# One-hot operands that interleave two tokens instead of four

## The chip, the cores and the metric

The kernel runs on one core of one Trainium2 chip. The metric is the device time of the program in microseconds (us). The kernel before took 1945.64 us, the median of three runs (1944.63 to 1948.22).

The engines are TensorE (PE in the profile, its weight loads PEld), VectorE (DVE), ScalarE (ACT), GpSimd (POOL) and the DMA queue of SyncE (SP).

## The reference

A decoder trunk of two layers on 256 tokens of 1024 columns, float32. Each layer has an attention mixer and then a PEER mixer, which takes most of the time. PEER works on product keys: 8 heads, for each two halves of 128 sub-keys, and 128 x 128 = 16384 experts of one neuron each.

```python
q = (xc @ w_q).reshape(t, PEER_HEADS, 2, PEER_QDIM // 2)
sc = jnp.einsum('thpc,hpnc->thpn', q, sub_keys).astype(jnp.float32)
v_half, i_half = lax.top_k(sc, PEER_TOPK_HALF)
...
top_s, pos = lax.top_k(cand, PEER_TOPK)
expert = jnp.take_along_axis(cand_idx, pos, axis=-1)
g = jax.nn.softmax(top_s, axis=-1)
u = u_tab[expert]
act = jax.nn.gelu(jnp.einsum('thkd,td->thk', u, xc).astype(jnp.float32), approximate=False)
w = (g * act).astype(xc.dtype)
return jnp.einsum('thk,thkd->td', w, v_tab[expert])
```

## The kernel before

The kernel does not gather experts. It multiplies the tokens with all 16384 rows of `u_tab`, applies gelu, multiplies by a dense matrix of gates that is zero where an expert was not chosen, and multiplies that with all of `v_tab`. An expert's number is (row, column) of a 128 x 128 table; the first half of the keys gives the row, the second the column.

`peer(layer, ...)` runs once per layer, in these stages:
- the queries: 16 tiles of `w_q`, each two halves of 12 matmuls in `split_prod` (L804 to L806), and the top-16 searches and the routing on VectorE (`stage1`, `stage2`);
- the u stage: 128 blocks `b` of 128 experts, each two halves of 12 matmuls of 256 columns (L804 to L806), into a PSUM tile `S`. `put_act` (L1010, L1011, L1013) takes a block from PSUM through gelu into the array `A`;
- the v stage: 128 blocks, 24 matmuls of 512 columns each (`mm`, L1072 to L1074).

All these products are in float32r, with every operand split in hi + lo: hi hi, lo hi and hi lo. The halves of the weights come through `Weights.split`: one DMA of 512 KB for two halves, then per half ScalarE rounds hi (L69) and VectorE subtracts for lo (L70), five buffers each.

The gate matrix is made in the generator `gates()`, whose steps `Background.pump` issues between the matmuls of the u stage. Each step handles four tokens, `t0` to `t0 + 3`, and its tiles come from the pool `ohp` with two buffers:
- `hot` builds four one-hot operands. `E` (bfloat16, tile `ohB`) is [128 slots, 2, 128 indices, 4 tokens]: the partition is one of the 128 (head, rank) slots of a token, the two planes are the one-hot of the row and of the column index. `G` (float16, tile `ohA`) has the row's one-hot times the two parts of the gate's mantissa, `RM`.
- VectorE compares `iotaX` with the indices in `R1` (L959 for both planes, L957 for the first alone) and multiplies (L963, L966; L970 for the gate's exponent). In every other step (`GA`) ScalarE makes the second plane, token by token: a square (L953) and a relu (L951).
- Then the gate products: for each of the four tokens and each of the two planes of `G` one matmul (L984), 128 columns of `G` against 128 columns of `E`, into a PSUM tile `scp`. This is a group of eight.
- ScalarE copies the result to `A` (L992), or VectorE multiplies it into blocks that `put_act` has already been to (L996).

The tokens are the innermost dimension of `E` and `G`, so that VectorE handles four neighbours with four different factors, and the columns of one token's operand lie four 2-byte elements, 8 bytes, apart. The gate groups lie in the u stage: 64 in each layer, 128 in all.

The program is recorded by a framework whose scheduler sets each engine's order when the kernel is built; the work is then in that order on each engine.

Of the kernel before, what the change touches and what calls it, by code (L numbers as in the profile page):

```python
# [38 lines left out]
class Weights:  # L39
    """The weights in the order of use: units of up to 1024 columns are loaded ahead of  # L40
    the products, and split in halves into float32r parts hi + lo = w."""
# [33 lines left out]
    def next(self, look=None):  # L75
        """the next half: (hi, lo)"""
        j = self.pos
        self.pos += 1
        self.split(j + (self.look if look is None else look))
        return self.parts.pop(j)  # L80

    def last4(self, products):
        """products(half, tb) of the next 4 halves (hi, lo): all for tb 0, then all for tb 1"""
# [10 lines left out]
class Background:  # L94
    """Streams of work (generators that yield the cost of each step) that is issued
    between the matrix products of the main stream."""
# [20 lines left out]
    def need(self, *names):  # L117
        """issue the streams of these names to their ends"""
# [25 lines left out]
def body(tc, I, out):  # L144
    nc = tc.nc
    with ExitStack() as ctx:
# [58 lines left out]
        iotaX = cp.tile([128, 128, 4], BF, name="iotaX")  # L205
        nc.vector.tensor_copy(iotaX, iota[:, :, None].to_broadcast([128, 128, 4]))
# [41 lines left out]
        def rsqrt(parts, n, name):  # L248
            """parts: columns [128, k] that add up to the sums of squares over n -> 1 / sqrt(mean + eps)"""
# [9 lines left out]
            # Newton's steps, y times -2, 16 and -8192 after them: y (3 - v y^2) / 2  # L259
# [10 lines left out]
        def x_rstd(scr, tbs=(0, 1)):  # L270
            """1 / rms of the tokens of the blocks tbs -> [128, len(tbs)]"""
# [12 lines left out]
        def to_T(src, c, col, hi, lo, psp, tag):  # L284
            """chunk c, src(tb, c) [128, 128] -> hi[c], lo[c] transposed, times the gain"""
# [7 lines left out]
        def product(hi, lo, cs, n, w, ps, first, last):  # L293
            """ps[tb] [128, n] += (hi+lo)[c][:, tb].T @ the half's chunks, c in cs"""
# [14 lines left out]
        def proj(name, hi, lo, chunks, n, per, psp, consume, pre=None):  # L309
            """one tile of n output columns; `per` chunks in each half"""  # L310
# [11 lines left out]
        def rope(dst, ps, nh, d, C_, S_, tb, tmpp):  # L322
            """dst [128, nh, d] = rope(ps [128, nh*d])"""
# [13 lines left out]
        def scaled(tables, r, ap, name):  # L337
            """rope tables times the tokens' factors r [128, 2]"""
# [8 lines left out]
        def attention(hs, qk, scale, vof, masks, ap, oT, psp, need1, need2):  # L347
            """a group of 4 heads. qk(h, qb, nk) -> (lhsT, rhs); vof(h, kc) -> V [128 keys, 64];
            oT (hi, lo): 8 chunks [128, 256]"""
# [78 lines left out]
        class OutProj:  # L428
            """x += (oT hi + lo).T @ w_out, chunk after chunk in the same accumulators"""
# [24 lines left out]
            def finish(self, cs):  # L454
                bg.need(*[f"A{c // 2 * 4}" for c in cs])
                """the last two chunks, and x += the sums"""
# [27 lines left out]
        def heads_T(dsts, tabs, psp, tmpp):  # L484
            """rope over 8 heads of 64 columns, then transposed to dsts = [(dst, scale, chunks)]"""
# [20 lines left out]
        # ---------------------------------------------------------------- layer 0 mixer  # L506
# [120 lines left out]
        # ---------------------------------------------------------------- layer 1 mixer  # L627
        def mla_mixer(gcol):
            with ExitStack() as c1:
# [28 lines left out]
                def put_c(j):  # L658
                    """columns 352j.. of [cq 768 | ckv 256 | kr 32]"""
# [28 lines left out]
                def put_heads(j, dst, tail, rname, out_):  # L688
                    """8 heads [t, 64 + 32] -> out_[j] [96, 8, 256]"""
# [54 lines left out]
        # ---------------------------------------------------------------- PEER  # L744
        def peer(layer, gcol, final=False):
            with ExitStack() as c1:
                pp = c1.enter_context(tc.tile_pool(name="pp", bufs=1))
                # the activations: the blocks from NA on take the place of the raw tokens
# [13 lines left out]
                R1, RM = hp.tile([128, 3, S], BF, name="R1"), hp.tile([128, 2, S], F16, name="RM")  # L762
# [19 lines left out]
                # the queries come from the raw tokens times the gain: 1 / rms goes to their scores  # L782
# [25 lines left out]
                def finish():  # L808
                    """the last norm, in the places of the loaded weights"""
# [15 lines left out]
                def top16(srcs, vals, idxs):  # L825
                    """the 16 largest of each source and their places, the sources in turn"""
# [17 lines left out]
                def stage2():  # L844
# [5 lines left out]
                    for tb in range(2):  # L850
                        v = V[:, tb].rearrange("p (h s) k -> p h s k", s=2)
                        # only pairs (a, b) with (a + 1)(b + 1) <= 16 can be among the 16 largest sums
# [13 lines left out]
                    # softmax over the 16; the first is the largest  # L866
# [3 lines left out]
                    for tb in range(2):  # L870
                        g, tpu = gs[:, tb], tps[:, tb]
                        iv = If[:, tb].rearrange("p (h s) k -> p h s k", s=2)
                        # place -> (a, b): the last row that starts at or before it
# [9 lines left out]
                        # (a + 1)(b + 1) - 1 pairs come before (a, b): the k-th has a and b up to k  # L883
# [31 lines left out]
                        nc.scalar.activation(R1[:, :2, ts], p[:, :2], AF.Copy)  # L915
# [3 lines left out]
                    # g = 2^e (m + r): m has 11 bits, r the rest  # L919
# [6 lines left out]
                    nc.scalar.activation(R1[:, 2], e2, AF.Copy)  # L926
# [10 lines left out]
                def gates():  # L937
                    def hot(t0, E, G):
                        t = slice(t0, t0 + 4)
                        bc = lambda r: r[:, None, t].to_broadcast([128, 128, 4])  # L940
# [5 lines left out]
                        def pair(i, relu):  # L946
                            if act:
                                for j in (i, i + 1):
                                    r = [RA[:, n, k + j:k + j + 1] for n in range(3)]
                                    if relu:  # L950
                                        nc.scalar.activation(e[:, :, j], e[:, :, j], AF.Relu, bias=r[1], scale=r[2])  # L951
                                    else:
                                        nc.scalar.activation(e[:, :, j], iota, AF.Square, bias=r[0], scale=-1.0)  # L953
# [200 lines left out]
```

## Time and profile before

| | us |
|---|---|
| median of three runs | 1945.64 |
| lowest, highest | 1944.63, 1948.22 |
| span of the profiled execution | 1945.3 |

The profiled execution has no time of its own beside the span; its span lies 0.3 us under the median of the runs.

The page's share of busy time is a mean over stages with different limits. The gate products lie between 322 and 628 us (layer 0) and between 1277 and 1582 us (layer 1); these two stretches are called gate stages below. Matmuls are pipelined, so their durations overlap: what a matmul costs in a row of others is read from the chain of waits, where each piece is the time from the end of the one before, and not from its own duration.

### The profile page before, as it was taken

To read this page: it belongs to the slowest core of one execution; us is meant where nothing else is said; L and a number is where in the kernel's file an instruction comes from. 1 tells how busy PE (TensorE), PEld (TensorE's weight loads), DVE (VectorE), ACT (ScalarE), POOL (GpSimd) and SP (SyncE) were. 2 spreads that over 40 slices of the span, in tenths; PEclk is the share of its full clock that TensorE was granted. 3 is DMA by queue.
4 is the path that set the end of the run, shared out by engine and by line. 5 is a ranking of instruction groups with operands and counts; after the bars stand their busy time and mean duration, and the time that the engine had idled before them with its cause. 6 is when DMAs were issued, how large, how long until landed. Compare 5 with 4: busy or idle time off the path is not lost.

```text
span 1945.3 us, 35740 instructions
## 1 busy us (share of the span) xinstructions
PE 1917.9 (99%) x12588; PEld 1727.7 (89%) x12588; DVE 1454.4 (75%) x3710; ACT 1264.2 (65%) x3060; POOL 6.4 (0%) x10
## 2 busy tenths in 40 slices
PE   8999999999999999999999999999999999999997
PEld 7769999999999888888888799999999998888886
DVE  7958998777788666666687699977778876666665
ACT  5556567887777555555576664688877765555554
POOL 0000000000000000000000000000000000000001
PEclk9989999999999999999999999999999999999999
DMA  6425565444444555555554345654444456666664
GB/s 186 128 65 164 172 195 166 154 151 152 152 152 153 194 192 190 192 192 190 189 168 131 120 150 177 195 163 152 144 152 152 154 171 191 190 194 193 188 193 141
DMA packets 90179, 323.33 MB, mean 166 GB/s; under 512 B 10512, under 2 KB 10896, under 8 KB 89744
## 3 DMA queue, kind: packets, MB, share of 16 engines
q1 hardware_dynamic: 88704, 318.71, 51.4%
q8 instruction: 99, 1.62, 0.3%
q0 software_dynamic: 288, 2.10, 0.3%
q14 instruction: 80, 0.66, 0.1%
q10 hardware_dynamic: 1008, 0.25, 0.1%
HBM read 319.97 MB, written 1.05 MB: 165 GB/s over the span
## 4 chain that ended last, share of the span: by engine, by line
PE 94%; DVE 3%; DMA 1%; ACT 1%; issue 1%; ACTq 0%; DVEq 0%
PE S L804 13%; PE S L805 13%; PE S L806 13%; PE acc L1072 12%; PE acc L1073 12%; PE acc L1074 12%; PE scp L984 6%; PE pj L301 2%; PE pj L303 2%; PE pj L302 2%; PE bk L372 1%; DVE lo L70 1%; DMA raw<-in_pu 1%; PE pj L438 1%; PE scp L1021 1%; PE pj L439 1%
## 5 line engine op out<-in xcount | busy, mean ns | idle before, releaser
L69 ACT ACTIVATE hi<-raw 128x512 fp32r<-128x512 f32 (+2 forms) x1214 | 763.2, 634 | 589.8 <-DVE lo L70 196.5
L70 DVE TENSOR_TENSOR lo<-raw,hi 128x512 fp32r<-128x512 f32 (+2 forms) x1214 | 827.1, 686 | 377.4 <-ACT hi L69 368.5
L804 PE MATMUL S<-hi,hi 128*128 128x256 f32 x2048 | 584.2, 285 | 1.9 <-ACT A L1013 1.8
L806 PE MATMUL S<-hi,lo 128*128 128x256 f32 x2048 | 573.4, 280 | 0.5 <-DVE lo L70 0.3
L805 PE MATMUL S<-lo,hi 128*128 128x256 f32 x2048 | 572.9, 280 | 0.0
L804 PEld LDWEIGHTS S<-hi,hi 128*128 128x128 f32 x2048 | 389.4, 190 | 3.1 <-ACT A L1013 2.9
L806 PEld LDWEIGHTS S<-hi,lo 128*128 128x128 f32 x2048 | 386.4, 189 | 1.3 <-DVE lo L70 1.2
L805 PEld LDWEIGHTS S<-lo,hi 128*128 128x128 f32 x2048 | 387.3, 189 | 0.0
L1073 PE MATMUL acc<-lo,ohA 128*128 128x512 f32 x512 | 200.2, 391 | 0.0
L1073 PE MATMUL acc<-lo,ohB 128*128 128x512 f32 x512 | 200.2, 391 | 0.0
L1074 PE MATMUL acc<-hi,ohA 128*128 128x512 f32 x512 | 199.4, 390 | 0.0
L1074 PE MATMUL acc<-hi,ohB 128*128 128x512 f32 x512 | 198.7, 390 | 0.0
L1072 PE MATMUL acc<-hi,ohB 128*128 128x512 f32 x512 | 160.5, 393 | 0.0
L1072 PE MATMUL acc<-hi,ohA 128*128 128x512 f32 x512 | 160.5, 393 | 0.0
L984 PE MATMUL scp<-ohA,ohB 128*128 128x128 f16 x1024 | 143.1, 296 | 0.0
L951 ACT ACTIVATE ohB<-ohB,RA 128x128 bf16<-128x128 bf16 x256 | 134.5, 654 | 0.0
L1074 PEld LDWEIGHTS acc<-hi,ohB 128*128 128x128 f32 x512 | 96.1, 188 | 22.0
L1074 PEld LDWEIGHTS acc<-hi,ohA 128*128 128x128 f32 x512 | 96.1, 188 | 22.0
L1072 PEld LDWEIGHTS acc<-hi,ohA 128*128 128x128 f32 x512 | 96.2, 188 | 20.8
L1072 PEld LDWEIGHTS acc<-hi,ohB 128*128 128x128 f32 x512 | 96.2, 188 | 20.7
L1073 PEld LDWEIGHTS acc<-lo,ohA 128*128 128x128 f32 x512 | 96.2, 188 | 20.3
L1073 PEld LDWEIGHTS acc<-lo,ohB 128*128 128x128 f32 x512 | 96.2, 188 | 20.2
(263 smaller groups left out, 2524.8 us busy)
## 6 DMA issues: line engine op xcount, KB each, us to landing
raw<-in_pu SPq DMA_DIRECT2D x256, 512.0 KB, 3.6
raw<-in_pv SPq DMA_DIRECT2D x256, 512.0 KB, 4.1
raw<-in_pq SPq DMA_DIRECT2D x32, 512.0 KB, 3.5
raw<-in_w SPq DMA_DIRECT2D x20, 512.0 KB, 3.7
raw<-in_uq SPq DMA_DIRECT2D x9, 512.0 KB, 4.3
raw<-in_w SPq DMA_DIRECT2D x12, 352.0 KB, 2.9
raw<-in_w0o SPq DMA_DIRECT2D x8, 512.0 KB, 3.6
raw<-in_w1o SPq DMA_DIRECT2D x8, 512.0 KB, 3.5
```

Of the source, the lines that this page charges most:

```text
L69: self.nc.scalar.activation(hi[:, :w], src, AF.Copy)
L70: self.nc.vector.tensor_tensor(lo[:, :w], src, hi[:, :w].bitcast(F32), op=OP.subtract)
L301: nc.tensor.matmul(ps[tb], hi[c][:, t], a, start=st, stop=False)
L302: nc.tensor.matmul(ps[tb], hi[c][:, t], b, start=False, stop=False)
L804: nc.tensor.matmul(p, a, hi[c], start=first and i == 0, stop=False)
L805: nc.tensor.matmul(p, a, lo[c], start=False, stop=False)
L806: nc.tensor.matmul(p, b, hi[c], start=False, stop=last and i == 3)
L951: nc.scalar.activation(e[:, :, j], e[:, :, j], AF.Relu, bias=r[1], scale=r[2])
L984: nc.tensor.matmul(p[:, i], E[:, 1, :, i], G[:, s, :, i], start=i + s == 0, stop=True, skip_group_check=True)
L1072: nc.tensor.matmul(o, a[:, 0, t], w[0], start=b == 0, stop=False)
L1073: nc.tensor.matmul(o, a[:, 0, t], w[1], start=False, stop=False)
L1074: nc.tensor.matmul(o, a[:, 1, t], w[0], start=False, stop=b == NK - 1)
```

## The change

The token dimension is cut in two: an operand is now [128 slots, 2 planes, 2 pairs, 128 indices, 2 tokens]. The two tokens of a pair are the innermost dimension, and the columns of one token's operand lie two elements, 4 bytes, apart. `iotaX` repeats every index twice instead of four times. The indices in `R1` are laid out by groups of four tokens, [64 groups, 2 planes, 4 tokens], so that plane and pair can be one dimension of the comparison; the exponent moves from `R1` to a tile of its own, `RE`. The count of every kind of instruction and the elements it handles stay, except for the cast that fills `iotaX`, which is half as large. The comments are left out of the changed file; its lines are 2 to 6 further on from L762 on (L984 is L990, L804 is L806).

```diff
-        iotaX = cp.tile([128, 128, 4], BF, name="iotaX")
-        nc.vector.tensor_copy(iotaX, iota[:, :, None].to_broadcast([128, 128, 4]))
+        iotaX = cp.tile([128, 128, 2], BF, name="iotaX")
+        nc.vector.tensor_copy(iotaX, iota[:, :, None].to_broadcast([128, 128, 2]))
...
-                R1, RM = hp.tile([128, 3, S], BF, name="R1"), hp.tile([128, 2, S], F16, name="RM")
+                R1 = hp.tile([128, S // 4, 2, 4], BF, name="R1")
+                RE, RM = hp.tile([128, S], BF, name="RE"), hp.tile([128, 2, S], F16, name="RM")
...
-                        nc.scalar.activation(R1[:, :2, ts], p[:, :2], AF.Copy)
+                        nc.scalar.activation(R1[:, tb * 32:(tb + 1) * 32].rearrange("p g s t -> p s g t"),
+                                             p[:, :2].rearrange("p s (g t) -> p s g t", t=4), AF.Copy)
...
-                    nc.scalar.activation(R1[:, 2], e2, AF.Copy)
+                    nc.scalar.activation(RE, e2, AF.Copy)
...
-                        t = slice(t0, t0 + 4)
-                        bc = lambda r: r[:, None, t].to_broadcast([128, 128, 4])
+                        pr = lambda r: r.rearrange("p (q t) -> p q t", t=2)[:, :, None, :]
+                        bc = lambda r: pr(r[:, t0:t0 + 4]).to_broadcast([128, 2, 128, 2])
+                        io = lambda n: iotaX[:, None].to_broadcast([128, n, 128, 2])
...
-                                        nc.scalar.activation(e[:, :, j], e[:, :, j], AF.Relu, bias=r[1], scale=r[2])
+                                        nc.scalar.activation(e[:, j // 2, :, j % 2], e[:, j // 2, :, j % 2], AF.Relu, bias=r[1], scale=r[2])
                                     else:
-                                        nc.scalar.activation(e[:, :, j], iota, AF.Square, bias=r[0], scale=-1.0)
+                                        nc.scalar.activation(e[:, j // 2, :, j % 2], iota, AF.Square, bias=r[0], scale=-1.0)
...
-                            nc.vector.tensor_tensor(E[:, 0], iotaX, bc(R1[:, 0]), op=OP.is_equal)
+                            nc.vector.tensor_tensor(E[:, 0], io(2), pr(R1[:, t0 // 4, 0]).to_broadcast([128, 2, 128, 2]),
+                                                    op=OP.is_equal)
                         else:
-                            nc.vector.tensor_tensor(E, iotaX[:, None].to_broadcast([128, 2, 128, 4]),
-                                                    R1[:, :2, None, t].to_broadcast([128, 2, 128, 4]), op=OP.is_equal)
+                            nc.vector.tensor_tensor(E.rearrange("p s q i t -> p (s q) i t"), io(4),
+                                                    pr(R1[:, t0 // 4].rearrange("p s t -> p (s t)")).to_broadcast([128, 4, 128, 2]),
+                                                    op=OP.is_equal)
...
-                            nc.vector.tensor_tensor(e, e, bc(R1[:, 2]), op=OP.mult)
+                            nc.vector.tensor_tensor(e, e, bc(RE), op=OP.mult)
...
-                            "p (s i t) -> p s i t", s=2, t=4) for n, d in (("ohB", BF), ("ohA", F16))]
+                            "p (s q i t) -> p s q i t", s=2, q=2, t=2) for n, d in (("ohB", BF), ("ohA", F16))]
...
-                                nc.tensor.matmul(p[:, i], E[:, 1, :, i], G[:, s, :, i], start=i + s == 0, stop=True,
+                                nc.tensor.matmul(p[:, i], E[:, 1, i // 2, :, i % 2], G[:, s, i // 2, :, i % 2], start=i + s == 0, stop=True,
```

What the scheduler makes of it is shown at three places. The first is VectorE in the gate stage of layer 0, before (`lo` is a half's low part, `scp` the PSUM tile of a gate group):

```order
L959 TENSOR_TENSOR ohB<-iotaX,R_1617 128x1024
L70 TENSOR_TENSOR lo<-raw,hi 128x512
L996 TENSOR_TENSOR A<-A,scp 128x40x4
L963 TENSOR_TENSOR ohA<-ohB,RM 128x512
L966 TENSOR_TENSOR ohA<-ohB,RM 128x512
L970 TENSOR_TENSOR ohB<-ohB,R_1617 128x512
L957 TENSOR_TENSOR ohB<-iotaX,R_1617 128x512
```

and the same place in the changed kernel:

```order
L964 TENSOR_TENSOR ohB<-iotaX,R_1617 128x1024
L70 TENSOR_TENSOR lo<-raw,hi 128x512
L1002 TENSOR_TENSOR A<-A,scp 128x40x4
L969 TENSOR_TENSOR ohA<-ohB,RM 128x512
L972 TENSOR_TENSOR ohA<-ohB,RM 128x512
L976 TENSOR_TENSOR ohB<-ohB,RE 128x512
L961 TENSOR_TENSOR ohB<-iotaX,R_1617 128x512
```

Nothing moved; the exponent's operand is RE. The second is TensorE at the first gate group, before (the group's other seven pairs follow):

```order
L805 MATMUL S<-lo_1631,hi 128x256
L806 MATMUL S<-hi_1623,lo 128x256
L804 MATMUL S<-hi_1624,hi 128x256
L805 MATMUL S<-lo_1632,hi 128x256
L806 MATMUL S<-hi_1624,lo 128x256
L984 LDWEIGHTS ohB
L984 MATMUL scp<-ohA,ohB 128x128
```

and in the changed kernel, where the names' numbers are one higher:

```order
L807 MATMUL S<-lo_1632,hi 128x256
L808 MATMUL S<-hi_1624,lo 128x256
L806 MATMUL S<-hi_1625,hi 128x256
L807 MATMUL S<-lo_1633,hi 128x256
L808 MATMUL S<-hi_1625,lo 128x256
L990 LDWEIGHTS ohB
L990 MATMUL scp<-ohA,ohB 128x128
```

The group stands behind the same product. The third is VectorE at the start of the program, as a difference (`ang` belongs to the rope tables, `lo_148` to `lo_151` to the transposed tokens of the first mixer):

```order
 L70 TENSOR_TENSOR lo<-raw,hi 128x400
-L206 CAST iotaX<-iota 128x512
-L232 SCALAR_TENSOR_TENSOR ang<-kk,ang 128x96
+L206 CAST iotaX<-iota 128x256
+L232 SCALAR_TENSOR_TENSOR ang<-kk,ang 128x96 x2
 L291 SCALAR_TENSOR_TENSOR lo_148<-bk,gains,hi_140 128x256
 L232 SCALAR_TENSOR_TENSOR ang<-kk,ang 128x96
 L291 SCALAR_TENSOR_TENSOR lo_149<-bk,gains,hi_141 128x256
```

The cast is half as large, and behind it the steps of the rope tables come somewhat earlier among the first products' operands; some matmuls of the first projection change places with it.

## Rows read from the trace of the kernel before

**Rows 1.** The page: busy time and share of each engine, and the clock granted to TensorE in 40 slices, in tenths.

```profile
PE 1917.9 (99%) x12588; PEld 1727.7 (89%) x12588; DVE 1454.4 (75%) x3710; ACT 1264.2 (65%) x3060; POOL 6.4 (0%) x10
...
PEclk9989999999999999999999999999999999999999
```

**Rows 2.** Windows: the stretch in us, its length, then busy us and instructions of PE, PEld, DVE, ACT, POOL, the granted clock, the DMA share and GB/s. The two gate stages, a stretch inside the first, and the v stage of layer 0.

```profile
322.00:628.00 306.00, 306.00 (x2614) 302.61 (x2613) 241.55 (x563) 241.63 (x713) 0.00 (x0) 1.00 0.48 152
1277.00:1582.00 305.00, 305.00 (x2605) 301.67 (x2604) 241.21 (x562) 240.58 (x711) 0.00 (x0) 1.00 0.48 152
...
550.00:580.00 30.00, 30.00 (x259) 29.68 (x258) 25.57 (x62) 23.83 (x69) 0.00 (x0) 1.00 0.46 151
...
640.00:930.00 290.00, 290.00 (x1269) 237.96 (x1268) 181.84 (x318) 165.75 (x318) 0.00 (x0) 1.00 0.59 192
```

**Rows 3.** The waits of the first gate stage, 322 to 628 us: who waited for whom, us in total, times, the longest.

```profile
ACT hi L69 <- PE S L805: 43.7, 73, 1.4
DVE lo L70 <- ACT hi L69: 34.8, 42, 1.8
DVE ohB L959 <- PE scp L984: 15.7, 16, 1.7
ACT A L992 <- PE scp L984: 10.5, 20, 0.9
DVE A L996 <- PE scp L984: 6.7, 11, 1.5
...
DVE ohB L957 <- PE scp L984: 5.4, 9, 1.0
```

**Rows 4.** The chain of waits: shares by line over the whole run and over 322 to 628 us, and three pieces of it (start, us, what) around the first gate group.

```profile
by line: PE S L804 12.8%; PE S L805 12.8%; PE S L806 12.7%; PE acc L1072 12.1%; PE acc L1073 11.9%; PE acc L1074 11.9%; PE scp L984 6.3%; PE pj L301 2.1%; PE pj L303 2.1%; PE pj L302 2.1%; PE bk L372 1.4%; DVE lo L70 1.1%; DMA raw<-in_pu 0.
...
by line: PE S L804 26.7%; PE S L805 26.7%; PE S L806 26.6%; PE scp L984 20.0%
...
322.14 0.12 PE S L806
...
322.61 0.96 PE scp L984 x8
323.57 0.12 PE S L804
```

**Rows 5.** Groups of instructions by line and shape: count, busy us, mean ns of one. A weight load over the whole run, and TensorE's matmuls of 322 to 628 us.

```profile
L805 PEld LDWEIGHTS S<-lo,hi 128*128 128x128 f32 x2048 | 387.3, 189 | 0.0
...
L804 PE MATMUL S<-hi,hi 128*128 128x256 f32 x701 | 201.2, 287 | 0.0
L805 PE MATMUL S<-lo,hi 128*128 128x256 f32 x701 | 196.3, 280 | 0.0
L806 PE MATMUL S<-hi,lo 128*128 128x256 f32 x700 | 196.1, 280 | 0.0
L984 PE MATMUL scp<-ohA,ohB 128*128 128x128 f16 x512 | 71.6, 296 | 0.0
```

**Rows 6.** The chain of waits in layer 1's attention: start, us, what. L374 adds a mask by a bfloat16 product with dense operands.

```profile
1040.80 0.22 PE bk L372 x2
1041.02 0.06 PE bk L374
1041.08 0.28 PE bk L372 x2
```

**Rows 7.** The instructions of two lines, with ns of the shortest, the median and the longest, first and last start in us; and from the timeline the eight weight loads of the first gate group (start, us).

```profile
L984 PEld LDWEIGHTS <-ohB x1024: 112/117/138, 322.4 to 1579.4; 128*128 128x128 bf16 x171
L984 PE MATMUL scp<-ohA,ohB x1024: 283/297/303, 322.5 to 1579.5; 128*128 128x128 f16 x171
...
L374 PEld LDWEIGHTS <-identb x64: 95/98/105, 72.5 to 1080.1; 128*128 128x128 bf16 x64
L374 PE MATMUL bk<-cnegb,identb x48: 219/221/289, 72.5 to 1080.4; 128*128 128x128 bf16 x48
...
322.45 0.82 PEld L984 LDWEIGHTS <-ohB 128*128 128x128 bf16 x8
```

**Rows 8.** Groups of VectorE's instructions by line and shape in 322 to 628 us.

```profile
L963 DVE TENSOR_TENSOR ohA<-ohB,RM 128x512 f16<-128x512 bf16 x62 | 26.0, 419 | 0.1
...
L959 DVE TENSOR_TENSOR ohB<-iotaX,R 128x1024 bf16<-128x1024 bf16 x31 | 21.4, 690 | 15.8 <-PE scp L984 15.7
L957 DVE TENSOR_TENSOR ohB<-iotaX,R 128x512 bf16<-128x512 bf16 x31 | 13.1, 421 | 5.5 <-PE scp L984 5.4
```

**Rows 9.** Instructions of two lines (ns of the shortest, median and longest): a float32 operation of VectorE on 512 elements, and the copy into R1; and the cast of iotaX in the chain of waits (start, us, what).

```profile
L893 DVE TENSOR_TENSOR A<-A x24: 681/685/709, 254.1 to 1265.0; 128x512 f32<-128x512 f32 x24
...
L915 ACT ACTIVATE R<-scp x4: 377/377/377, 290.3 to 1270.0; 128x256 bf16<-128x256 f32 x4
...
9.64 0.42 DVE iotaX L206
```

**Rows 10.** ScalarE: four squares in a stream from the timeline (start, us), and the group of the copies from PSUM.

```profile
325.87 1.47 ACT L953 ACTIVATE ohB<-iota,RA 128x128 bf16<-128x128 f32 x4
...
L992 ACT ACTIVATE A<-scp 128x96 f32<-128x96 f32 x48 | 12.6, 263 | 0.6 <-PE scp L984 0.5
```

**Rows 11.** TensorE's waits in the first 150 us, after that for its first load.

```profile
PE pj L301 <- ACT hi L290: 2.1, 1, 2.1
```

## The prediction

> **What bounds the kernel now.** I read the busy shares first. TensorE is busy for 99% of the span, its granted clock is 9 tenths or more in all slices but one, and VectorE and ScalarE have 75% and 65% [rows 1]. A share alone does not say that TensorE sets the time, so I cut the span at the first and the last gate product of each layer: 322 to 628 us and 1277 to 1582 us. [...] The waits of the first stage confirm it: TensorE is in none of them, and the other two wait for TensorE, ScalarE for 43.7 + 10.5 = 54.2 us and VectorE for 15.7 + 6.7 + 5.4 = 27.8 us [rows 3]. So in these stages a nanosecond less of matmul is a nanosecond less of time, until one of the others is full.
>
> The chain of the stage tells what a gate product costs. L984 holds 20.0% of 306 us, 61.2 us for 512 matmuls: 119.5 ns each; a group of eight is 0.96 us, and the matmul behind it goes on at 0.12 us [rows 4, 5]. Over the whole run that is 128 groups x 0.957 = 122.5 us, the 6.3% of the whole chain [rows 4]. The same chain gives 80.0% to L804 to L806: 244.8 us for 2102 matmuls, 116.5 ns each, though these stream 256 columns where a gate product streams 128 [rows 4, 5]. A gate product thus costs per column twice what its neighbours do.
>
> **The change part by part.** *The columns of the gate products.* The eight matmuls of a group stay; their operands' columns come 4 bytes apart instead of 8. Two kinds of product show what other distances cost. L374 multiplies dense bf16 (2 bytes apart) and holds 0.06 us of the chain, half of a gate product; the pair of L372 behind it takes 0.28 us instead of 0.22, because its 32-bit weights are loaded behind the short product [rows 6]. The float32 products have columns exactly 4 bytes apart, the new distance. L1072 to L1074 stream 512 of them in 290 / 1269 = 228.5 ns [rows 2], L804 to L806 256 in 116.5 ns: 112 ns for 256 more columns, so 128 fewer than 256 leaves 116.5 - 56 = 60.5 ns. Both ways agree on about 60 ns. The weight load has room for that pace as far as rows tell: at 8 bytes it lasts 117 ns, dense 98 ns [rows 7]. The load of a float32 product lasts 189 ns [rows 5] at a pace of 116.5, so some 72 ns of a load lie beside the product it serves and the one before; 98 - 72 leaves 26 ns.
>
> The new group is 8 x 60.5 = 484 ns plus 56 ns for the first float32 load behind it, 540 ns, against 957: 417 ns less. Times 128 that is 53.4 us. The bounds: nothing gained (119.5 ns, the row of today), and at most the streaming alone, 128 x 112 / 256 = 56 ns without the loss behind, 957 - 448 = 509 ns a group, 65 us. I take 53.4, between the two rows that lie next to the new distance.
>
> [...]
>
> *The VectorE operations of a group.* Their counts and sizes stay; runs of four equal-stride elements become runs of two. Today 512 16-bit elements take 419 ns, 1024 take 690 [rows 8]: 271 ns for 512 more, where 512 float32 elements take 685 in all, 266 more than 512 16-bit ones [rows 9]. So VectorE handles two 16-bit elements in the time of one of float32, and a run of two is still one whole step. I take no change. The bound on the other side is one element a step, 685 - 419 = 266 ns more for 512; the bound below is nothing, since two a step is the best that any such row shows. The cover is VectorE's idle time, 306 - 241.6 = 64.4 us in a stage today [rows 2] and 306 - 26.7 - 241.6 = 37.7 us in a stage shortened by 53.4 / 2.
>
> *The ScalarE squares and relus* (L953, L951) write, and the relus read, elements 4 bytes apart instead of 8. Today four squares in a stream take 1.47 us, 368 ns each; the nearest row with dense elements is L992, 96 of them in 263 ns [rows 10]. Bounds: 368 - 263 = 105 ns less each, or as much more, 256 of them a stage, 27 us of ScalarE either way. Both ends stay under ScalarE's idle time, 306 - 241.6 = 64.4 us today [rows 2] and 37.7 us in the shortened stage, so TensorE hides them. I take nothing.
>
> *The rest.* The copies of the routing numbers into R1 (L915, four in the run, 377 ns each [rows 9]) write runs of four elements now; doubled they would be 1.5 us of ScalarE more, beside products. The cast of iotaX halves: 0.42 us, and it lies on the chain of the start [rows 9]; half of it would be 0.2 us. Around it the scheduler orders some two dozen early instructions otherwise; I price that at 0 with 2 us to either side, the longest wait of TensorE there apart from the first load (2.1 us) [rows 11]. In the gate stages each engine's instructions stand as before. SP's queue is untouched; the stage draws 152 GB/s, 167 when 27 us shorter, under the 192 of the next stage [rows 2].
>
> *What is late next.* With 279 us a stage both other engines stand at 241.6 / 279 = 87%. Their work is uneven: VectorE has 25.6 of 30 us between 550 and 580 [rows 2], 93% of the shortened stretch. I allow 1 us of new TensorE waits over both stages. Sum: 1945.3 - 53.4 - 0.2 + 1 = 1892.7 against the profiled span. The median of the runs shown is 0.3 us above that span, so 1893.
>
> **The rivals.** *The weight load sets the pace.* No row of 16-bit loads with their products goes on faster than 119.5 ns each in the trace; the 60 ns come from a single dense product among others [rows 6]. If a load can't hide behind a product of 60 ns, the pace ends between 60 and the dense load's whole 98 ns [rows 7]; at the middle, 79 ns, a group is 8 x 79 + 38 (the float32 load behind waits 116.5 - 79) = 670 ns, 287 less, 37 us in all: 1909. At 98 ns it is 8 x 98 + 18 = 802, 155 less, 20 us: 1926. For it speaks that the load starts only when the product before starts (eight loads take 0.82 us [rows 7]); against it that the float32 load of 189 ns fits a pace of 116.5. [...] This case has a chance of 0.15.
>
> *Nothing changes on TensorE*, because 16-bit columns are quick only where they are dense and 4 bytes cost as much as 8: 1945. That L374 alone shows the 60 ns speaks for it, the float32 rows at exactly 4 bytes speak against it [rows 2, 4]. [...] This case has 0.07.
>
> *ScalarE or VectorE fills up.* If half the gain turns into waits at 87% load, 1919. The 27.8 and 54.2 us that they wait for TensorE now [rows 3], each more than a stage's 26.7 us, speak against it. Chance 0.07.
>
> *VectorE drops to one element a step* in its runs of two: L963 and L966 64 times a layer, L957 and L970 32 times, L959 32 times at double size, 256 x 0.266 = 68 us more. VectorE's busy time becomes 310 us in a stage that lasts 306 today and would last 279. VectorE is then the bound, and the gain is gone with 4 us more per stage: 1953; up to 35 us of its waits for ScalarE [rows 3] per stage could come on top. It ends slower from 64.4 us, 252 of the 266 ns per 512 elements; from 37.7 us (147 ns) on it only eats the gain. Against it speaks that a pair is one step. Chance 0.05.
>
> **How the numbers follow.** The forecast has 0.66, with 1888 to 1899 as its own range: 60 ns shifted by 5 ns moves 8 x 128 x 5 = 5 us, and the start adds 2. The pace of 79 ns lies at 1909, the half-lost gain at 1919, no change at 1945. Reaching from 1886 to 1920 leaves out about 0.2: the cases of no change and of a slower kernel (0.12), the slow ends of the weight load and of the filled engines (0.06) and a tail below (0.02). About 0.2%, 4 us, is what a measurement of this kernel can tell from no change. Faster: 0.66 + 0.15 + 0.07 = 0.88; same: 0.07; slower: 0.05.
>
> **What would show it.** Right: in the chain of the stage, the groups of eight gate products at some 0.5 us instead of 0.96, a stage of about 279 us, the gate product's own duration down from 297 towards the 221 ns of L374 [rows 7], VectorE's operations still at 419 and 690 ns. Wrong: groups at 0.65 to 0.8 us (load), at 0.96 (nothing), waits of TensorE on L957, L966 or L951 (the others full), or 685 ns where 419 stood.

## The result, and the profile after

The changed kernel takes 1881.12 us (median of 4 runs, 1880.58 to 1883.49) against 1946.91 us before (4 runs, 1944.63 to 1948.22): a ratio of 0.967, with a 95% interval of 0.9656 to 0.9684. The forecast was 1893, in a range from 1886 to 1920: the direction was right, the time is 12 us below the forecast, and it lies 5 us below the range. The profiled spans are 1945.3 and 1879.2 us, 66.1 us apart.

The page after, as in [rows 1]:

```profile
PE 1852.2 (99%) x12588; PEld 1664.2 (89%) x12588; DVE 1447.2 (77%) x3710; ACT 1247.3 (66%) x3060; POOL 6.4 (0%) x10
...
PEclk9989999999999999999999999999999999999999
```

TensorE's busy time falls by 65.7 us, nearly the whole gain, and VectorE's by 7. The windows, with the columns of [rows 2]: the two gate stages, now 271 us long, and the v stage of layer 0.

```profile
322.00:593.00 271.00, 271.00 (x2585) 268.59 (x2583) 235.63 (x556) 229.94 (x704) 0.00 (x0) 1.00 0.53 170
1243.00:1514.00 271.00, 271.00 (x2583) 268.58 (x2581) 235.64 (x557) 229.83 (x704) 0.00 (x0) 1.00 0.53 170
640.00:930.00 290.00, 290.00 (x1269) 237.96 (x1268) 181.62 (x317) 166.17 (x318) 0.00 (x0) 1.00 0.59 191
```

In both gate stages TensorE is still busy from end to end at clock 1.00, with VectorE at 87% and ScalarE at 85%. The v stage has the same 1269 matmuls in 290 us as before. The waits of the first gate stage (321.8 to 593.2 us), as in [rows 3]:

```profile
ACT hi L69 <- PE S L807: 33.6, 69, 0.9
DVE lo L70 <- ACT hi L69: 24.3, 34, 1.6
DVE ohB L964 <- PE scp L990: 9.5, 11, 1.2
...
ACT A L998 <- PE scp L990: 1.7, 6, 0.4
```

TensorE is in no row of this view. What the others wait for it has shrunk from 43.7 to 33.6 us at L69 and from 15.7 to 9.5 us at the one-hot comparison: slack was used up, not exceeded.

The chain of waits of the stage and three pieces of it (start, us, what), as in [rows 4]. L984 is L990 now, and L804 to L806 are L806 to L808.

```profile
by line: PE S L806 30.3%; PE S L807 29.3%; PE S L808 29.2%; PE scp L990 11.2%
...
321.92 0.47 PE scp L990 x8
322.39 0.17 PE S L806
322.56 0.12 PE S L807
```

A group holds 0.47 us instead of 0.96, and the first float32 matmul behind it 0.17 instead of 0.12. The two lines of the product itself, as in [rows 7] (ns of the shortest, the median and the longest):

```profile
L990 PEld LDWEIGHTS <-ohB x1024: 96/97/101, 321.8 to 1513.6; 128*128 128x128 bf16 x171
L990 PE MATMUL scp<-ohA,ohB x1024: 218/218/233, 321.8 to 1513.6; 128*128 128x128 f16 x171
```

And the groups of VectorE and ScalarE in the stage, as in [rows 8]; L955 is the relu, L957 the square (behind the bar: busy us of all together, mean ns of one):

```profile
L969 DVE TENSOR_TENSOR ohA<-ohB,RM 128x512 f16<-128x512 bf16 x62 | 25.9, 418 | 0.1
...
L964 DVE TENSOR_TENSOR ohB<-iotaX,R 128x1024 bf16<-128x1024 bf16 x31 | 21.3, 687 | 9.5 <-PE scp L990 9.5
L961 DVE TENSOR_TENSOR ohB<-iotaX,R 128x512 bf16<-128x512 bf16 x31 | 13.0, 419 | 0.8 <-PE scp L990 0.6
...
L955 ACT ACTIVATE ohB<-ohB,RA 128x128 bf16<-128x128 bf16 x124 | 56.9, 525 | 0.0
L957 ACT ACTIVATE ohB<-iota,RA 128x128 bf16<-128x128 f32 x124 | 40.8, 436 | 0.0
```

The relu and the square of the kernel before, from 322 to 590 us:

```profile
L951 ACT ACTIVATE ohB<-ohB,RA 128x128 bf16<-128x128 bf16 x112 | 59.3, 655 | 0.0
L953 ACT ACTIVATE ohB<-iota,RA 128x128 bf16<-128x128 f32 x112 | 41.1, 567 | 0.9 <-PE scp L984 0.6
```

**Where the 66.1 us are.** I added up the distances from the start of each matmul to the start of the next, from the first gate product of a stage to the last. The stage falls from 302.75 to 271.08 us, in both layers alike. Of these 31.7 us the groups (from their first product to the first float32 matmul behind them, and up to them) are 62.9 - 36.0 = 26.9, the matmuls that follow an interruption 13.5 - 13.1 = 0.4, and the remaining 1943 distances between float32 neighbours 226.4 - 222.1 = 4.3 us. Twice that is 53.8 + 0.8 + 8.6 = 63.2 (63.3 unrounded). The other 2.8 us lie outside of the gate stages: 0.7 us ahead of the first, and 1.7 us between the first query product of layer 1 and the first gate product there. Among the kernels below the first gate product starts anywhere from 321.6 to 328.1 us, and that stretch of layer 1, 171.1 us after and 172.8 before, takes from 170.8 us up, so I put no cause to them.

The 4.3 us are the part that the forecast did not have. The neighbours' distances are not spread around 116.5 ns, the mean used in the forecast: they take one of two values, about 113.4 ns and about 117.8 ns, and keep it over long runs. Before, 566 of the 1943 (0.29) were short; after, 1534 (0.79). Their mean went from 116.5 to 114.3 ns. This raised two questions: which part of the edit makes the group faster, and what sets the neighbours' pace.

### The profile page after: what moved, and what is told of

It is laid out like the page before. It is cut to its first block, busy times and chain, and to the rows that moved or that the text cites. A ratio compares the mean times of both kernels' runs of the same rounds, so it can differ in the third digit from the quotient of the medians.

```text
span 1879.2 us, 35739 instructions
## 1 busy us (share of the span) xinstructions
PE 1852.2 (99%) x12588; PEld 1664.2 (89%) x12588; DVE 1447.2 (77%) x3710; ACT 1247.3 (66%) x3060; POOL 6.4 (0%) x10
## 3 DMA queue, kind: packets, MB, share of 16 engines
q1 hardware_dynamic: 88704, 318.71, 52.6%
## 4 chain that ended last, share of the span: by engine, by line
PE 92%; DVE 6%; ACT 1%; issue 1%; DMA 0%; ACTq 0%; DVEq 0%
PE S L806 13%; PE S L807 13%; PE S L808 13%; PE acc L1079 12%; PE acc L1080 12%; PE acc L1078 12%; PE scp L990 3%; PE pj L301 2%; PE pj L303 2%; PE pj L302 2%; DVE lo L70 2%; PE bk L372 1%; DVE A L834 1%; DVE A L831 1%; DVE A L838 1%; PE pj L438 1%
## 5 line engine op out<-in xcount | busy, mean ns | idle before, releaser
L69 ACT ACTIVATE hi<-raw 128x512 fp32r<-128x512 f32 (+2 forms) x1214 | 756.0, 628 | 566.6 <-DVE lo L70 198.0
L806 PE MATMUL S<-hi,hi 128*128 128x256 f32 x2048 | 579.3, 283 | 1.8 <-ACT A L1019 1.8
L808 PE MATMUL S<-hi,lo 128*128 128x256 f32 x2048 | 568.9, 278 | 0.4
L806 PEld LDWEIGHTS S<-hi,hi 128*128 128x128 f32 x2048 | 386.0, 188 | 2.6 <-ACT A L1019 2.6
L808 PEld LDWEIGHTS S<-hi,lo 128*128 128x128 f32 x2048 | 384.7, 188 | 1.2 <-DVE lo L70 1.1
L955 ACT ACTIVATE ohB<-ohB,RA 128x128 bf16<-128x128 bf16 x256 | 117.2, 525 | 0.0
L957 ACT ACTIVATE ohB<-iota,RA 128x128 bf16<-128x128 f32 x256 | 84.1, 435 | 0.0
```

The source lines that it names most:

```text
L69: self.nc.scalar.activation(hi[:, :w], src, AF.Copy)
L806: nc.tensor.matmul(p, a, hi[c], start=first and i == 0, stop=False)
L808: nc.tensor.matmul(p, b, hi[c], start=False, stop=last and i == 3)
L955: nc.scalar.activation(e[:, j // 2, :, j % 2], e[:, j // 2, :, j % 2], AF.Relu, bias=r[1], scale=r[2])
L957: nc.scalar.activation(e[:, j // 2, :, j % 2], iota, AF.Square, bias=r[0], scale=-1.0)
```

## The experiments

All but dense_write change or add gate products alone; the diffs show only the lines that tell the kernels apart. In the first eight the product reads other places of the same tiles, through one of these views (of a tile with the old or the new interleaving, `i` being the token):

```
four    p i t -> (i t) -> q i t, q=2, t=2: [:, i // 2, :, i % 2]    columns 4 bytes apart
eight   (q i t) -> i t, t=4:               [:, :, i]                columns 8 bytes apart
dense   (i t):                             [i * 128:(i + 1) * 128]  columns 2 bytes apart
sixteen (s i t) -> i t, t=8:               [:, :, i]                columns 16 bytes apart
```

The first four ask which operand, and whether the writes matter.

```diff
 r4_both, from the kernel before
-  nc.tensor.matmul(p[:, i], E[:, 1, :, i], G[:, s, :, i], ...
+  nc.tensor.matmul(p[:, i], four(E[:, 1], i), four(G[:, s], i), ...
 r4_moving, from the kernel before
+  nc.tensor.matmul(p[:, i], E[:, 1, :, i], four(G[:, s], i), ...
 r4_weights, from the kernel before
+  nc.tensor.matmul(p[:, i], four(E[:, 1], i), G[:, s, :, i], ...
 r8_both, from the kernel after
-  nc.tensor.matmul(p[:, i], E[:, 1, i // 2, :, i % 2], G[:, s, i // 2, :, i % 2], ...
+  nc.tensor.matmul(p[:, i], eight(E[:, 1], i), eight(G[:, s], i), ...
```

> The kernel before, with all writes as before (four tokens interleaved, elements written 8 bytes apart); only the gate products read their columns 4 bytes apart, so they read other tokens' elements and the gates come out as other numbers. Theory A (all of the gain lies in what TensorE reads, the float32 neighbours' faster pace too): groups of eight 0.48 us, L804 to L806 near 114.5 ns each in the gate stages, 1881 us. Theory B (the neighbours are faster because ScalarE and VectorE write 4 bytes apart and disturb less): groups 0.48 us, but the neighbours stay at 116.6 ns: 1890 to 1892 us.

> The kernel before; only the moving operand (G) is read 4 bytes apart, the weights (E) stay at 8 bytes (gates come out as other numbers). If the moving operand's read sets the gate product's pace: groups about 0.48 us, 1880 to 1893 us. If the weight load's read does: 0.96 us, 1946 us.

> The kernel before; only the weights (E) are read 4 bytes apart, the moving operand (G) stays at 8 bytes (gates come out as other numbers). If the moving operand's read sets the pace: groups stay at 0.96 us and the time at 1946 us, the load's own duration falls from 117 to about 97 ns. If the weight load does: 0.48 us, 1880 to 1893 us.

> The changed kernel with all its writes 4 bytes apart; only the gate products read their columns 8 bytes apart again (gates come out as other numbers). Theory A: groups 0.96 us, neighbours back at 116.6 ns, 1946 us. Theory B: groups 0.96 us, neighbours stay at 114.5 ns: about 1935 us.

Measured, against 1947.59 us of the kernel before in the same job: r4_both 1884.47 (4 runs; ratio 0.9682, interval 0.9666 to 0.9698), r4_moving 1891.79, r4_weights 1948.79, r8_both 1948.19. The instructions of the product, r4_moving first:

```profile
L987 PE MATMUL scp<-ohA,ohB x1024: 217/221/253, 322.2 to 1524.5; 128*128 128x128 f16 x171
```

and r4_weights:

```profile
L987 PE MATMUL scp<-ohA,ohB x1024: 276/296/300, 323.8 to 1581.3; 128*128 128x128 f16 x171
```

The gain follows the reads of TensorE: the old writes with reads at 4 bytes have it (r4_both), the new writes with reads at 8 bytes have none of it (r8_both). And it follows the moving operand: with this one alone at 4 bytes the product lasts 221 ns, with the weights alone 296, beside 297 in [rows 7]. In r4_moving a weight load lasts 113 ns and the products start 60 ns apart (medians), so a load longer than the pace hides, at 2.1 us a stage more in the groups than with both operands at 4 bytes. r4_both also keeps ScalarE's old writes; its squares last 571 ns against 436 in the kernel after, and its gate stage of layer 0 is 271.1 us as in the kernel after, so ScalarE's gain is hidden. The neighbours' pace goes with the reads, too: r4_both and the kernel after, with different writes, have the same pace at each of the 1943 distances of that stage, and r8_both has the share of the kernel before, 0.29.

The next four ask how the price goes on with the distance, and whether a product pays for itself alone.

```diff
 r2_both, from the kernel before
+  nc.tensor.matmul(p[:, i], dense(E[:, 1], i), dense(G[:, s], i), ...
 r16_both, from the kernel before
+  nc.tensor.matmul(p[:, i], sixteen(E, i), sixteen(G, i + 4 * s), ...
 one8_last, from the kernel after
+  nc.tensor.matmul(p[:, i], E[...], eight(G[:, s], i) if 2 * i + s == 7 else G[...], ...
 one8_mid, from the kernel after
+  nc.tensor.matmul(p[:, i], E[...], eight(G[:, s], i) if 2 * i + s == 3 else G[...], ...
```

> The kernel before with its writes; the gate products read dense columns, 2 bytes apart, in both operands (gates come out as other numbers). If 4 bytes is already the full pace: 58 ns a product and groups of 0.47 us as in the changed kernel, about 1881 us, up to 9 us more if the float32 neighbours keep their slower pace. If denser is faster still: groups clearly under 0.45 us, under 1878 us.

> The kernel before with its writes; the gate products read columns 16 bytes apart in both operands (gates come out as other numbers). If the pace goes on with the distance (58 ns at 4 bytes, 118 at 8): some 235 ns a product, groups near 1.9 us, 128 x 0.94 = 120 us more than before: 2065 us. If there are only two paces, near and far: 0.96 us, 1946 us.

> The changed kernel; of each group's eight products only the last reads its moving operand 8 bytes apart (gates come out as other numbers). It costs 60 ns more, but the first float32 product behind it no longer waits 55 ns for its weights: 0.6 us over the run. If the product that ends a group sets the pace of the float32 products behind it, these go back towards 116.6 ns: 1881 + 9 = 1890 us. If it does not, they stay at 114.5: 1882 us.

> The changed kernel; of each group's eight products only the fourth reads its moving operand 8 bytes apart (gates come out as other numbers). It costs 60 ns a group, 7.7 us. If the end of a group sets the neighbours' pace: 114.5 ns as in the changed kernel, 1889 us. If any product at 8 bytes does, or the group's length: another share of the slow pace, up to 1898 us.

Measured: r2_both 1909.61, r16_both 2060.66, one8_last 1910.64, one8_mid 1916.20; the kernel before in this job 1944.94. r16_both came out near what was expected; the other three are 18 to 21 us slower than the slowest time expected of them. Their groups are not the reason (the last three rows belong to kernels further below):

| kernel | time, us | products start apart, ns (median) | groups, us a stage | short distances | gate stage, us | v stage, mean ns of a matmul |
|---|---|---|---|---|---|---|
| before (8 bytes) | 1946.91 | 118 | 62.9 | 0.29 | 302.8 | 228.9 |
| after (4 bytes) | 1881.12 | 58 | 36.0 | 0.79 | 271.1 | 228.9 |
| r4_both | 1884.47 | 58 | 36.0 | 0.79 | 271.1 | 228.9 |
| r4_moving | 1891.79 | 60 | 38.1 | 0.47 | 275.9 | 228.9 |
| r4_weights | 1948.79 | 116 | 61.8 | 0.00 | 304.0 | 228.9 |
| r8_both | 1948.19 | 118 | 62.9 | 0.29 | 302.8 | 228.9 |
| r2_both (2 bytes) | 1909.61 | 56 | 35.4 | 0.04 | 277.0 | 233.3 |
| r16_both (16 bytes) | 2060.66 | 234 | 116.3 | 0.88 | 358.4 | 228.9 |
| one8_last | 1910.64 | 57 | 36.1 | 0.01 | 278.3 | 233.3 |
| one8_mid | 1916.20 | 58 | 39.9 | 0.18 | 280.2 | 233.3 |
| nudge_first | 1883.80 | 58 | 36.0 | 0.79 | 271.2 | 228.9 |
| r2_nudge | 1896.69 | 56 | 35.5 | 0.04 | 277.1 | 228.9 |
| r2_nine | 1887.10 | 56 | 38.8 | 0.85 | 273.6 | 228.9 |

(Groups, share and gate stage are of layer 0; the stage of layer 1 differs by at most 0.8 us, and in most kernels by less than 0.1; the share there by at most 0.09. The share is of the 1943 distances between neighbours in the stage, 1941 in r2_nine.)

So the price of a product is 56 ns at 2 bytes, 58 at 4, 118 at 8 and 234 at 16: nearly flat from 2 to 4 bytes, then about in proportion to the distance up to the 16 bytes tried. The two operands were told apart at 4 and 8 bytes only; at 2 and 16 both moved. It is paid by the product that has the distance: one product at 8 bytes in the middle of a group adds (39.9 - 36.0) / 64 = 61 ns to it, and as the last one of a group it adds 0.1 us a stage: the group's piece of the chain grows from 0.47 to 0.53 us, and that of the float32 matmul behind it falls from 0.17 to 0.12 us. What made these kernels slow is in the last three columns: most distances between neighbours long, 5 to 7 us a stage more than in the kernel after, and 1535 matmuls of each v stage at 233.3 instead of 228.9 ns, 6.9 us a stage, although no gate product runs there. The two paces in the chain, at the same time of the run: 21 matmuls of the kernel after,

```profile
400.01 0.11 PE S L806
...
402.28 0.11 PE S L808
402.39 0.47 PE scp L990 x8
402.87 0.17 PE S L806
403.04 0.12 PE S L807
403.16 0.11 PE S L808
```

and 21 of r2_both:

```profile
399.97 0.12 PE S L804
...
402.33 0.12 PE S L806
402.44 0.46 PE scp L987 x8
402.91 0.17 PE S L804
403.08 0.12 PE S L805
403.20 0.12 PE S L806
```

From the first start to the last it is 2.27 us, 113.5 ns each, and 2.36 us, 118 ns each, on the same operation and shape; behind this group each goes on as it came. Both have clock 1.00 there. The next kernels ask whether that pace belongs to the distance of the columns or to the point at which a group lets the stream go on. Each adds products whose sum the next one overwrites. A third question goes with them: what the remaining step, to dense columns, costs VectorE.

```diff
 nudge_first, from the kernel after (r2_nudge: the same from r2_both, with t0 == S - 4 and
 the dense views)
+  if t0 == 0:
+      nc.tensor.matmul(p[:, 0], E[:, 1, 0, :, 0], G[:, 0, 0, :, 0], start=True, stop=True, ...
   for i in range(4):
 dense_write, from the kernel after (iotaX, the comparisons, the squares and the relus follow the new layout)
-  pr = lambda r: r.rearrange("p (q t) -> p q t", t=2)[:, :, None, :]
-  bc = lambda r: pr(r[:, t0:t0 + 4]).to_broadcast([128, 2, 128, 2])
+  pr = lambda r, n: r[:, :, None].to_broadcast([128, n, 128])
+  bc = lambda r: pr(r[:, t0:t0 + 4], 4)
...
-  "p (s q i t) -> p s q i t", s=2, q=2, t=2
+  "p (s t i) -> p s t i", s=2, t=4
...
-  nc.tensor.matmul(p[:, i], E[:, 1, i // 2, :, i % 2], G[:, s, i // 2, :, i % 2], ...
+  nc.tensor.matmul(p[:, i], E[:, 1, i], G[:, s, i], ...
```

> The kernel after, with one gate product more ahead of the first group of each layer; the next product overwrites its sum, so the output stays. Theory A, the float32 neighbours' pace is handed on from one interruption to the next: the product itself costs 58 ns a layer and the groups stay at 36.0 us a stage, but the neighbours behind the first group may fall into the other of their two paces and keep it; if they do, a gate stage moves from 271.1 us to between 269 and 279, the v stage from 351.3 to 358.2, and the time to 1890 to 1910; if they do not, 1881. Theory B, each spacing has its own pace for the neighbours: 1881, every stage within 0.2 us of the kernel after.

> The kernel with dense reads, with one gate product more ahead of the last group of each layer, overwritten by the next. As there, the products read other elements than their own tokens'. Theory A, the pace is handed on: the first gate stage repeats 277.0 us up to its last group, and the v stage behind it either keeps 358.2 us or falls to 351.3; if it falls in both layers, 1896, else 1910. Theory B, dense reads slow the stages themselves: 277.0 and 358.2 us in both layers, 1910.

> The whole computation with one token's 128 columns dense, written so by VectorE and ScalarE, whose operations then repeat one number along the innermost run. Theory A, VectorE does two 16-bit elements a step only where no operand repeats one element along the run: 512 elements take 685 ns instead of 418, VectorE has 68 us more a layer, 304 us in a gate stage that lasts 271, and the stage ends at 305 to 330 us: 1950 to 2000. Theory B, a repeated element is as fast as a pair: 418 and 690 ns as before, group products 56 ns apart, 1878 with the neighbours at the fast pace, 1908 at the slow one.

Measured, beside 1947.24 us of the kernel before: nudge_first 1883.80, r2_nudge 1896.69, dense_write 1969.45.

nudge_first tells nothing apart: the stream behind the group with the added product has the same pace as without it, and the stage is 0.1 us longer, about the product itself. r2_nudge does: it has one product more than r2_both in each layer, 56 ns of work, and is 12.9 us faster. Its gate stage repeats r2_both's within 0.06 us, and its v stages run at the other pace. The v stage of layer 0, r2_both:

```profile
640.00:930.00 290.00, 290.00 (x1245) 234.89 (x1244) 177.88 (x311) 162.88 (x312) 0.00 (x0) 1.00 0.59 188
```

and r2_nudge, with 24 matmuls more in the same 290 us:

```profile
640.00:930.00 290.00, 290.00 (x1269) 237.95 (x1268) 181.66 (x317) 166.18 (x318) 0.00 (x0) 1.00 0.59 192
```

The last kernel puts the added product ahead of every group.

```diff
 r2_nine, from r2_nudge
-  if t0 == S - 4:
-      nc.tensor.matmul(p[:, 0], dense(E[:, 1], 0), ...
+  nc.tensor.matmul(p[:, 0], dense(E[:, 1], 0), ...
```

> The kernel with dense reads, with one gate product more ahead of every group, overwritten by the next: 128 products more, 56 ns each, 7.2 us. As there, the products read other elements than their own tokens'. Theory A, the point at which a group lets go of the stream decides the neighbours' pace, whatever the spacing: the share of the short distances in the gate stages leaves 0.04, and the v stage is 351.3 us as with the one added product; with a share of 0.8 a stage is 277.0 + 3.6 - 6.5 = 274 us and the time 1889; with 0.04 in the stages and only the v stage changed, 1902. Theory B, dense reads have the long pace by themselves: the share stays at 0.04, the v stage at 358.2, and the time is 1909.6 + 7.2 = 1917.

Measured: 1887.10 us, 128 products more than r2_both and 22.5 us faster; the kernel before in this job 1944.19. The share of short distances goes from 0.04 to 0.85 with every column as far from the next as in r2_both. The same stretch of its chain, 400.07 to 402.56 us, has 22 distances: 113.2 ns each.

```profile
400.07 0.11 PE S L806
...
402.56 0.11 PE S L804
402.75 0.45 PE scp L989 x8
403.20 0.17 PE S L805
```

So neither the distance of the columns nor the stream's own operands set the pace: with both as they were, an added product changes it. These kernels ran once each, and not all on one chip; chance or the chip do not explain the difference, for r2_nudge, on another chip than r2_both, repeats its pace at each of the 1943 distances of the first gate stage. The distances also show when the pace is chosen: in each of the 132 to 134 stretches of float32 matmuls behind gate products, both stages together, in all kernels of the table, it settles within four distances between neighbours and then stays to the next. Over a v stage it stays, too, but the step from the u to the v stage can change it: in the kernel before the u stage ends at 118 ns, the long pace, and the v stage runs at 228.9, the short one.

dense_write shows where the slow VectorE of the prediction's fourth rival comes. VectorE's groups:

```profile
L972 DVE TENSOR_TENSOR ohA<-ohB,RM 128x512 f16<-128x512 bf16 x64 | 43.7, 684 | 0.0
...
L964 DVE TENSOR_TENSOR ohB<-iotaX,R 128x1024 bf16<-128x1024 bf16 x31 | 37.8, 1220 | 3.0 <-PE scp L990 2.7
```

and its gate stage, in the columns of the windows, with TensorE's waits in it:

```profile
328.00:639.00 311.00, 289.68 (x2588) 283.54 (x2587) 297.96 (x556) 231.56 (x702) 0.00 (x0) 0.97 0.46 148
...
PE S L806 <- ACT A L1019: 15.6, 11, 2.5
PE scp L990 <- DVE A L1002: 5.5, 2, 3.1
```

Dense columns, with a gate product of 219 ns (median) as in r2_both, do not help here: VectorE needs 684 ns where it needed 418 and is busy for 298 of 311 us, 96%. TensorE idles for 21 us of the stage and has a granted clock of 0.97 over it. Most of the idle time, 15.6 us, is a wait for ScalarE, which frees a block's PSUM tile (L1019, in `put_act`); that ScalarE is late there because of VectorE was not tested. The scheduler also puts some instructions in another order, and its part in the 40 us that the stage is longer than in the kernel after was not separated. The pair of tokens that the change keeps together is in any case worth its 2 ns a product.

## Why the prediction was right, and where it was wrong

The direction and the mechanism of the gain were right; one row of the sum was taken for a fixed price but moved, and this put the time below the range.

*TensorE bounds the gate stages:* right. [rows 2] has it busy without a break in both, and it has no wait in them after the change, either.

*The group:* right. 540 ns were forecast; the chain shows 475 ns and 55 ns more for the float32 matmul behind, 530. The gain is 427 ns x 128 = 54.7 us where the working had 53.4, and 54.6 by the distances above. The product starts every 58 ns where 60.5 was derived from the float32 rows at 4 bytes. That working took one row at its short pace (228.5) and one as a mean of two paces (116.5); with both short, 228.9 and 113.4, it gives 56 ns, with both long, 233.3 and 117.8, 60. The experiments bear out the reason, distance of the columns in what TensorE reads, and narrow it to the moving operand.

*VectorE:* right. 418, 419 and 687 ns against 419, 421 and 690, and no wait of TensorE on it.

*ScalarE taken at nothing:* right for the time, and the bound holds. One square alone fell from 567 to 436 ns and one relu from 655 to 525, but in a stream they overlap, and the bound of 105 ns was on the busy time of a stream: this fell from 41.1 / 112 = 367 to 40.8 / 124 = 329 ns a square, 38 less, and from 59.3 / 112 = 529 to 56.9 / 124 = 459 a relu, 70 less. TensorE hides it.

*What is late next:* the 1 us of new waits did not come.

*The step that failed* is the chain's row of 116.5 ns for the neighbours, L804 to L806, which the sum kept as a fixed price and left out of the range. It was a mean of two paces, and the change moved the mix: the row measured 114.3 ns, 8.6 us less in the two gate stages. Without these 8.6 us the time would have been 1889.7, inside the range. With the 1 us of waits that did not come, 1.3 us more of the group and 2.8 us outside of the stages less the 0.2 of iotaX, that is the 13.5 us between the forecast sum of 52.6 and the measured 66.1. Bounds for the gate stages could have been had from before's own trace: 1943 distances at 113.4 instead of 116.5 ns are 6.0 us a stage, at 117.8 2.5 us more. That the v stages can go up by 6.9 us each, as in three of the kernels here, only the experiments showed. A range that took these in would have reached from 1893 - 12 = 1881 to 1893 + 5 + 14 = 1912 on this term alone.

*The rivals.* The weight load does not set the pace: in r4_moving loads of 113 ns stand beside products 60 ns apart. In the kernel after, the products go on at 58 ns in groups of eight; the longest row of them in any run here is nine, in r2_nine, at 56 ns. "Nothing changes" falls with the measured product: 58 ns at 4 bytes against 118 at 8. The engines that fill up did not: 87% and 85%, and TensorE waits for neither. VectorE at one element a step did not come with runs of two, where 512 elements take 418 ns; dense_write shows its duration, 684 ns for the 685 given, with one number repeated along the run, in a kernel that ends slower than before, 1969.45 against 1947.24.

**What stays open.** Why the float32 stream has two paces, and what at the end of a group selects one, is not shown; neither the distance of the columns (2 bytes give 0.04 and 0.85) nor the length of the group (36.0 us a stage give 0.79, 36.1 give 0.01) predicts it here. Nor is it shown whether a kernel could be led to the short pace throughout: all short would be 222.1 - 1943 x 0.1134 = 1.8 us less in each gate stage of the kernel after. No kernel tried here beats the kernel after.

## What to carry to other kernels

Look at the distance between the columns that a matmul streams: in these runs 4 bytes cost little more than 2 (58 and 56 ns a product), and each of the two doublings beyond about doubled the product (118 and 234 ns); from 8 to 4 bytes it was the moving operand that counted. Here it was enough that the writer keeps pairs together, at no cost, and full density cost more on the writing engine than it saved: VectorE's 684 instead of 418 ns. Before a row's mean enters a sum as a price that the change does not touch, look at its distribution: a mean of two values is a term of its own, with bounds from both. And a single edit around a tight stream should be judged by the stage and by the line it aims at as well as by the total, since a product of 56 ns moved the total by 12.9 us here.

## What the runs showed of the hardware that was not expected

- Float32 matmuls of 256 columns follow each other at about 113.4 or about 117.8 ns, those of 512 at 228.9 or 233.3 ns, at clock 1.00, with the same shapes and tiles; the pace settles within four distances behind a group of gate products and holds to the next, in each of the 132 to 134 stretches of a kernel; one product more in every group took the share of short distances from 0.04 (r2_both) to 0.85 (r2_nine).
- The price of the operands' distance is nearly flat from 2 to 4 bytes (56 and 58 ns for 128 columns) and about doubles at each of the two doublings measured after it, to 8 and 16 bytes (118, 234 ns); from 8 to 4 bytes the moving operand alone brings it to 60 ns, the weights alone to 116.
- ScalarE's squares, with 16-bit outputs, get shorter with the distance, too: of 128 elements, 567 to 571 ns at 8 bytes, 431 to 436 at 4, 391 dense. In a stream, where they overlap, the busy time of one falls less: 367, 329 and 321 ns.
- VectorE on 512 16-bit elements took 418 ns with runs of two tokens and 684 ns where one operand repeats a single number along the run (dense_write).
